# Layer 1 attention: mask, sink and row minimum in one VectorE instruction, no mask matmuls, exponential in place

## The chip, the cores and the metric

One core of a Trainium2 chip runs the whole program. The metric is the device time in microseconds (us) of one execution. The time before is the median of three runs; one further execution was taken with a profile, and its rows are the ones shown here.

## The reference, cut to what matters

Two layers work on 1024 latent tokens and 256 context tokens. The part that is changed is the attention of layer 1, for the latent tokens alone: 16 query heads share 4 key heads (64 wide), each block of 128 queries sees the 256 context tokens and a band of at most three blocks of 128 latent tokens, and every head has one more logit, the sink, that takes part in the softmax but has no value.

```python
valid = (jnp.abs(qpos[:, None] - kpos[None, :]) <= WINDOW) & (kpos[None, :] >= 0) & (kpos[None, :] < n)
s_loc = jnp.einsum('bqkgd,bskd->bkgqs', qi, kb).astype(jnp.float32) * scale
s_loc = jnp.where(valid, s_loc, -1e30)
s_ctx = jnp.einsum('bqkgd,bskd->bkgqs', qi, kc).astype(jnp.float32) * scale
p = jax.nn.softmax(jnp.concatenate([s_ctx, s_loc, sink_col], axis=-1), axis=-1).astype(v.dtype)
return (jnp.einsum('bkgqs,bskd->bqkgd', p[..., :L_ctx], vc)
        + jnp.einsum('bkgqs,bskd->bqkgd', p[..., L_ctx:L_ctx + 3 * BLOCK], vb))
```

## The kernel before

The attention is cut into 32 units: 8 query blocks (`i`) times 4 key heads (`kv`), and a unit has 4 query heads (`h`). In the 24 units of blocks 1 to 6 the band is three blocks wide, so that a head has 640 score columns; in the 8 units of blocks 0 and 7 it has 512.

The steps of a unit are short methods. `Q` transposes the queries on TensorE and `Qh` copies them to SBUF. `S` computes the scores of a head into PSUM: two products for the context columns, two for the band (the query is split in a high and a low part that lie under each other, and so are two versions of the keys), and then one or two products of the identity with a 128x128 mask `mkb` (0 or -1e30), which are accumulated onto the first and the last 128 band columns. `mx` takes the negated maximum of the scores (VectorE, reads PSUM) and then the minimum of that and the negated sink, in a 128x1 instruction. `e` is the exponential on ScalarE, from PSUM into the SBUF tile `P`, with the negated maximum as its bias and the row sum as a second output. `T` and `V` transpose `P` on TensorE; `hi` (ScalarE) and `lo` (VectorE) split the transposed tile into a high and a low part, `pt`; for the fifth 128 columns these steps are `vh` and `vl`. `AV` multiplies by the values, block by block, into one PSUM tile `po`, of which there is one buffer. `ob` and `ot` copy its two halves out (ScalarE), `ad` adds them (GpSimd), `se`, `ee` and `sum` make the reciprocal of the softmax's sum, `N` spreads it over 64 partitions by TensorE, and `mu` multiplies (VectorE).

The order of these steps is written out by hand: `SWA_ORDER` lists 45 steps with a shift each, and in every step of the loop the steps of the present unit (shift 0), the one before (1), and so on, are issued in that order. So every engine has a fixed queue, and the units overlap. A query block's `q_block` loads the queries (SyncE) and splits them on GpSimd (a copy of 1.0 us and a subtraction of 2.4 us); it is issued once in four units. Score tiles have two PSUM buffers, the small transposes two, `po` and the spread reciprocal one each. The tile `P` has five buffers, which the loads of keys and values at the stage's start use as well (`ks`).

Ahead of the units, ten tiles of keys and values are loaded and split, `mk` (the two masks) is loaded by one transfer and rounded to bf16 by ScalarE, and the sink is loaded and negated (`nsink`).

Of the kernel before, what the change touches and what calls it, by code (L numbers as in the profile page):

```python
# [9 lines left out]
F32 = mybir.dt.float32  # L10
QUEUES = {mybir.EngineType.PE, mybir.EngineType.Activation, mybir.EngineType.DVE, mybir.EngineType.Pool, mybir.EngineType.SP}
F32R = mybir.dt.float32r
BF16 = mybir.dt.bfloat16
I32 = mybir.dt.int32
U32 = mybir.dt.uint32
AF = mybir.ActivationFunctionType
ALU = mybir.AluOpType
AX = mybir.AxisListType
# [5 lines left out]
NC = 256  # L24
NT = NX + NC
TC = NC // 128
TX = NX // 128
# [70 lines left out]
def hybrid_block_kernel(ctx, tc, A, out, dbg=None, upto=99):  # L98
    nc = tc.nc
    dbg = dbg or {}  # L100
    pe, act, dve, pool, sp = nc.tensor, nc.scalar, nc.vector, nc.gpsimd, nc.sync
# [20 lines left out]
    def bank(tag, name):  # L122
        bufs, banks = cur["tags"][tag]
        return cur["p"].tile([128, 512 * banks], F32, tag=tag, bufs=bufs, name=name)
# [8 lines left out]
    identb = const.tile([128, 128], BF16, name="identb")  # L133
# [29 lines left out]
    def hilo(hi, lo, src):  # L163
        act.copy(hi, src)
        dve.tensor_sub(lo, src, hi.bitcast(F32))  # L165
# [580 lines left out]
    def layer0_mixer():  # L746
# [20 lines left out]
        with sbuf("l0a") as ap_, sbuf("l0t") as tp:  # L767
# [127 lines left out]
            with sbuf("l0b") as bp, psum("l0s", S=(2, 2), M=(1, 1), T=(2, 1), O=(1, 1)):  # L895
                class Pair:


                    def __init__(self, h, g):
                        self.h, self.g = h, g  # L900
                        self.mxm = bp.tile([128, 2], F32, tag="mx", bufs=4, name="mx")
                        self.sm = [bp.tile([128, 3], F32, tag="sm", bufs=8, name="sm") for _ in range(2)]
                        self.P, self.Sb, self.last, self.PT = {}, {}, {}, None

# [26 lines left out]
                    def probabilities(self, u):  # L931
                        if u not in self.P:
                            self.P[u] = bp.tile([128, NT], F32, tag="P", bufs=3, name="P")
                        return self.P[u]

# [13 lines left out]
                    def T(self, u, c):  # L949
# [5 lines left out]
                        for j in range(n):  # L955
                            pe.transpose(p[:, j * 128:(j + 1) * 128], self.P[u][:, (b0 + j) * 128:(b0 + j + 1) * 128], ident)  # L956
                        us = slice(u * 128, (u + 1) * 128)
# [38 lines left out]
                class Few(Pair):  # L996


                    def __init__(self, h):
                        self.h, self.g = h, 0  # L1000
                        self.mxm, self.sms = [bp.tile([128, 2], F32, tag=t, bufs=2, name=t) for t in ("fmx", "fsm")]
                        self.P = bp.tile([128, 2, NC], F32, tag="fP", bufs=1, name="fP")
                        self.PT = [bp.tile([128, TC, 256], F32R, tag=f"fpt{i}", bufs=1, name=f"fpt{i}") for i in range(2)]
# [940 lines left out]
    def layer1_mixer(st1, last, load_qkv, w_qkv, cols, x_first):  # L1944
# [199 lines left out]
        with sbuf("l1a") as ap_, sbuf("l1k", side="right") as kp, psum("l1s", S=(2, 2), B=(2, 1), O=(1, 1), R=(1, 1)):  # L2144
            kT = [ap_.tile([128, 4, NT], F32R, name=f"k1T{i}") for i in range(2)]
            V = []
            for t in range(TT):
                ks = ap_.tile([128, 640], F32, tag="P", bufs=5, name="ks1")[:, :512].rearrange("p (i h d) -> p i h d", i=2, d=64)
                sp.dma_start(ks, kvd[t * 128:(t + 1) * 128])
                v = ap_.tile([128, 4, 2, 64], F32R, name=f"V1_{t}")  # L2150
                pool.tensor_copy(v[:, :, 0, :], ks[:, 1])
                pool.tensor_sub(v[:, :, 1, :], ks[:, 1], v[:, :, 0, :].bitcast(F32))
                V.append(v)
                kk = ap_.tile([128, 5, 4, 128], F32R, tag=f"pt{t % 2}", bufs=2, name="kk")
                kk = kk.rearrange("p a b c -> p (a b c)")[:, :768].rearrange("p (a b c) -> p a b c", a=4, c=64)
                hilo(kk[:, :, 0, :], kk[:, :, 1, :], ks[:, 0])
                dve.tensor_copy(kk[:, :, 2, :], kk[:, :, 0, :].bitcast(F32))
                ts = slice(t * 128, (t + 1) * 128)
                for i in range(2):
                    p = bank("B", "pkt")  # L2160
                    for j in range(4):
                        pe.transpose(p[:, j * 128:(j + 1) * 128].bitcast(F32R),
                                     kk[:, j, i:i + 2, :].rearrange("p i d -> p (i d)"), identr)
                    (act.copy if i else dve.tensor_copy)(kT[i][:, :, ts], p.rearrange("p (h t) -> p h t", t=128))
            mk = kp.tile([128, 2, 128], F32, name="mk")
            sp.dma_start(mk, A["band"].rearrange("m p s -> p m s"))
            mkb = ap_.tile([128, 2, 128], BF16, name="mkb")
            act.copy(mkb, mk)
            sinkb = ap_.tile([128, 16], F32, name="sinkb")
            load_bcast(sinkb, A["swa_sink"], 0, 16)  # L2170
            nsink = ap_.tile([128, 16], F32, name="nsink")
# [12 lines left out]
            class Unit:  # L2184
# [18 lines left out]

                def Qh(self):
                    self.qT = ap_.tile([128, 4, 128], F32R, tag="qT", bufs=2, name="qT1")
                    act.copy(self.qT, self.qp.rearrange("p (h t) -> p h t", t=128))

                def S(self, h):
                    i, kv, nl, l0 = self.i, self.kv, self.nl, self.l0
                    p = self.Sb[h] = bank("S", "psc1")  # L2210
                    pc, pl = p[:, NC:512], p[:, 512:512 + nl]
                    q = self.qT[:, h, :]
                    for n in range(2):
                        pe.matmul(pc, q, kT[1 - n][:, kv, :NC], start=n == 0, stop=n == 1)
                    for n in range(2):
                        pe.matmul(pl, q, kT[1 - n][:, kv, l0:l0 + nl], start=n == 0, stop=False)
                    ms = ([(0, 0)] if i > 0 else []) + ([(1, nl - 128)] if i < TX - 1 else [])
                    for n, (w, c0) in enumerate(ms):
                        pe.matmul(pl[:, c0:c0 + 128], identb, mkb[:, w, :], start=False, stop=n == len(ms) - 1)

                def mx(self, h):
                    hd = self.kv * 4 + h
                    nm = self.nm[:, h:h + 1]
                    dve.tensor_reduce(nm, self.Sb[h][:, NC:NC + self.nk], axis=AX.X, op=ALU.max, negate=True)
                    dve.tensor_tensor(nm, nm, nsink[:, hd:hd + 1], op=ALU.min)

                def e(self, h):
                    P = self.P[h] = ap_.tile([128, 640], F32, tag="P", bufs=5, name="P1")
                    act.activation(P[:, :self.nk], self.Sb[h][:, NC:NC + self.nk], AF.Exp, bias=self.nm[:, h:h + 1],
                                   accum_out=self.sm[:, h:h + 1])  # L2230

                def T(self, h):
                    p = bank("B", "ppt1")
# [77 lines left out]
            with tc.manual_schedule():  # L2311
                q_block(0)
                for step in range(len(units) + depth):
# [8 lines left out]
                    for name, shift in SWA_ORDER:  # L2322
                        p = obj.get(step - shift)
# [62 lines left out]
    if upto < 5.5:  # L2386
        return
    pre = layer1_mixer(st1, lasts[0], load_qkv, w_qkv, cols, x_first)
    if upto < 7:
        return  # L2390
# [167 lines left out]
```

## Time and profile before

| | before |
|---|---|
| median of 3 runs | 2895.5 us (2894.02 to 2897.7) |
| the profiled execution | 2898.11 us, its span 2896.3 us |
| TensorE matmuls, share of the span | 92% |
| VectorE | 76% |
| ScalarE | 56% |
| GpSimd | 16% |
| first score product of layer 1's attention, last mask product | 1832.8 us, 2102.3 us |

The shares are means over stages with different limits, so what the change is worth must be read from its own stage, which takes about 9% of the span. The profiled execution took 2.6 us more than the median of the runs; differences worked out from its rows are taken off the median.

### The profile page before, as it was taken

To read this page: it belongs to the slowest core of one execution; us is meant where nothing else is said; L and a number is where in the kernel's file an instruction comes from. 1 tells how busy PE (TensorE), PEld (TensorE's weight loads), DVE (VectorE), ACT (ScalarE), POOL (GpSimd) and SP (SyncE) were. 2 spreads that over 40 slices of the span, in tenths; PEclk is the share of its full clock that TensorE was granted. 3 is DMA by queue.
4 is the path that set the end of the run, shared out by engine and by line. 5 is a ranking of instruction groups with operands and counts; after the bars stand their busy time and mean duration, and the time that the engine had idled before them with its cause. 6 is when DMAs were issued, how large, how long until landed. Compare 5 with 4: busy or idle time off the path is not lost.

```text
span 2896.3 us, 43462 instructions
## 1 busy us (share of the span) xinstructions
PE 2677.9 (92%) x16939; PEld 2152.5 (74%) x16939; DVE 2200.8 (76%) x3425; ACT 1620.5 (56%) x2443; POOL 449.8 (16%) x294
## 2 busy tenths in 40 slices
PE   7999899999879999999999899899988599999996
PEld 5989899987657777776767677688866488877775
DVE  4776799986776666666676586899966688888887
ACT  4201577773245555555555543689933476676664
POOL 2100000000012110201111300322101522221103
PEclk8999999999989999999999899799989799999998
DMA  7552000017468878787878374311056699999994
GB/s 269 195 176 95 5 9 10 10 61 251 143 226 311 297 266 288 277 283 279 296 271 290 133 268 149 114 45 36 16 192 241 212 383 383 383 381 377 368 354 144
DMA packets 277198, 614.44 MB, mean 212 GB/s; under 512 B 25320, under 2 KB 73184, under 8 KB 274944
## 3 DMA queue, kind: packets, MB, share of 16 engines
q1 hardware_dynamic: 261840, 567.91, 54.6%
q0 software_dynamic: 15008, 43.62, 5.7%
q8 instruction: 133, 2.18, 0.3%
q14 instruction: 73, 0.60, 0.1%
q10 hardware_dynamic: 144, 0.13, 0.0%
HBM read 549.94 MB, written 61.67 MB: 211 GB/s over the span
## 4 chain that ended last, share of the span: by engine, by line
PE 71%; DVE 7%; ACT 6%; issue 2%; DMA 1%; POOL 1%; SPq 0%; DVEq 0%; ACTq 0%; POOLq 0%
PE pw L1226 6%; PE pg L1786 4%; PE pu L1788 4%; PE pu L1789 4%; PE pu L1791 4%; PE pd L1878 4%; PE pd L1874 4%; PE pg L1790 4%; PE pg L1787 4%; PE pd L1875 4%; ACT wh L1100 3%; PE po L982 3%; PE po L2285 2%; PE ppt L956 2%; PE ptr L410 2%
## 5 line engine op out<-in xcount | busy, mean ns | idle before, releaser
L1101 DVE TENSOR_TENSOR wl<-raw,wh 128x2048 fp32r<-128x2048 f32 x385 | 868.2, 2282 | 293.6 <-ACT wh L1100 292.4
L1100 ACT CAST wh<-raw 128x2048 fp32r<-128x2048 f32 (+1 forms) x392 | 734.3, 1903 | 338.5 <-PE pg L1790 203.1
L1883 POOL DMA_INDIRECT acc_x<-yo,gp x30 | 116.4, 3879 | 695.1 <-DVE yo L1882 653.1
L1788 PE MATMUL pu<-wl,xh 128*128 128x512 f32 x512 | 204.3, 399 | 6.0 <-DVE wl L1101 5.9
L1786 PE MATMUL pg<-wl,xh 128*128 128x512 f32 x512 | 208.6, 407 | 0.0
L1787 PE MATMUL pg<-wh,xh 128*128 128x512 f32 x512 | 202.9, 396 | 0.0
L1791 PE MATMUL pu<-wh,xl 128*128 128x512 f32 x512 | 202.0, 395 | 0.0
L1790 PE MATMUL pg<-wh,xl 128*128 128x512 f32 x512 | 202.0, 394 | 0.0
L1789 PE MATMUL pu<-wh,xh 128*128 128x512 f32 x512 | 201.9, 394 | 0.0
L1874 PE MATMUL pd<-wl,hh 128*128 128x512 f32 x480 | 194.0, 404 | 3.7 <-ACT csl L1817 3.7
L1875 PE MATMUL pd<-wh,hh 128*128 128x512 f32 x480 | 192.0, 400 | 0.0
L1878 PE MATMUL pd<-wh,hl 128*128 128x512 f32 x480 | 150.8, 395 | 0.0
L168 PE MATMUL pc<-hT,wh 128*128 128x256 f32 x480 | 140.2, 292 | 5.5 <-ACT wh L503 3.7
L170 PE MATMUL pc<-hT,wl 128*128 128x256 f32 x480 | 137.6, 287 | 4.8 <-DVE wl L504 4.8
L169 PE MATMUL pc<-hT,wh 128*128 128x256 f32 x480 | 136.5, 284 | 0.0
L1786 PEld LDWEIGHTS pg<-wl,xh 128*128 128x128 f32 x512 | 96.5, 188 | 36.3 <-issue 12.5
L1788 PEld LDWEIGHTS pu<-wl,xh 128*128 128x128 f32 x512 | 96.5, 189 | 33.4 <-DVE wl L1101 11.8
L1795 ACT ACTIVATE sil<-pg 128x512 f32<-128x512 f32 x64 | 38.3, 599 | 144.7 <-PE pg L1790 144.7
L1811 PE MATMUL pcg<-raw,cT 128*32 128x256 f32 x2048 | 116.9, 380 | 0.1
L963 ACT CAST pt<-ppt 128x512 fp32r<-128x512 f32 (+1 forms) x192 | 95.0, 515 | 39.1 <-PE ppt L956 37.0
L967 DVE TENSOR_TENSOR pt<-ppt,pt 128x512 fp32r<-128x512 f32 (+1 forms) x192 | 110.6, 593 | 7.7 <-ACT pt L963 5.2
L1790 PEld LDWEIGHTS pg<-wh,xl 128*128 128x128 f32 x512 | 96.5, 188 | 23.2 <-DVE xl L165 0.4
(459 smaller groups left out, 6592.0 us busy)
## 6 DMA issues: line engine op xcount, KB each, us to landing
raw<-in_exp_w_gate_dram SPq DMA_DIRECT2D x128, 1024.0 KB
raw<-in_exp_w_up_dram SPq DMA_DIRECT2D x128, 1024.0 KB
raw<-in_exp_w_down_dram SPq DMA_DIRECT2D x128, 1024.0 KB
raw<-in_mod_w_dram SPq DMA_DIRECT2D x48, 1024.0 KB
yT<-yTd SPq DMA_DIRECT2D x17, 512.0 KB
acc_x<-xn SPq DMA_DIRECT2D x16, 512.0 KB
h2x<-h SPq DMA_DIRECT2D x16, 512.0 KB
raw<-in_w_in_dram SPq DMA_DIRECT2D x8, 768.0 KB
```

The lines of the kernel that those rows point to most:

```text
L1100: act.copy(wh[:, cs], raw[:, cs])
L1101: (eng or dve).tensor_sub(wl[:, cs], raw[:, cs], wh[:, cs].bitcast(F32))
L1226: pe.matmul(self.pp[n], a[:, k], b[k // 2][:, k % 2, ns], start=(k == 0 and i == 0), stop=(k == 7 and i == 2))
L1786: pe.matmul(pg, xh[:, k], gl[:, j], start=k == 0, stop=False)
L1787: pe.matmul(pg, xh[:, k], gh[:, j], start=False, stop=False)
L1788: pe.matmul(pu, xh[:, k], ul[:, j], start=k == 0, stop=False)
L1789: pe.matmul(pu, xh[:, k], uh[:, j], start=False, stop=False)
L1790: pe.matmul(pg, xl[:, k], gh[:, j], start=False, stop=k == 7)
L1791: pe.matmul(pu, xl[:, k], uh[:, j], start=False, stop=k == 7)
L1874: pe.matmul(pd[n], hh[k // 4][:, k % 4], w[2][:, k % 2, ns], start=k == 0, stop=False)
L1875: pe.matmul(pd[n], hh[k // 4][:, k % 4], w[1][:, k % 2, ns], start=False, stop=False)
L1878: pe.matmul(pd[n], hl[k // 4][:, k % 4], w[1][:, k % 2, ns], start=False, stop=k == 7)
```

## The change

The queries are copied to SBUF with a factor of -1, so that the scores are negated. The mask products are gone. `mx` is one call: it adds the negated mask (an f32 tile in SBUF that is 0 over all unmasked columns and 1e30 where masked) to the negated scores in PSUM, writes the sum to `P` in SBUF, and gives the minimum over the row and the negated sink. `e` is the exponential of the negated `P`, in place. `P` is therefore taken one step earlier, and has six buffers. Two masks are made ahead of the units (640 and 512 columns; block 0 takes the shorter one, block 7 the first 512 columns of the longer one): GpSimd zeroes, three transfers load the two triangles, GpSimd negates.

```diff
-                ks = ap_.tile([128, 640], F32, tag="P", bufs=5, name="ks1")[:, :512].rearrange("p (i h d) -> p i h d", i=2, d=64)
+                ks = ap_.tile([128, 640], F32, tag="P", bufs=6, name="ks1")[:, :512].rearrange("p (i h d) -> p i h d", i=2, d=64)
...
-            mk = kp.tile([128, 2, 128], F32, name="mk")
-            sp.dma_start(mk, A["band"].rearrange("m p s -> p m s"))
-            mkb = ap_.tile([128, 2, 128], BF16, name="mkb")
-            act.copy(mkb, mk)
+            masks = [kp.tile([128, 640 - 128 * n], F32, name=f"mask{n}") for n in range(2)]
+            for n, m in enumerate(masks):
+                pool.memset(m[:, :NC + 256 - 128 * n], 0.0)
+                sp.dma_start(m[:, NC + 256 - 128 * n:], A["band"][1])
+            sp.dma_start(masks[0][:, NC:NC + 128], A["band"][0])
+            for m in masks:
+                pool.tensor_scalar(m[:, NC:], m[:, NC:], -1.0, None, op0=ALU.mult)
...
-                    act.copy(self.qT, self.qp.rearrange("p (h t) -> p h t", t=128))
+                    act.activation(self.qT, self.qp.rearrange("p (h t) -> p h t", t=128), AF.Copy, scale=-1.0)
...
-                        pe.matmul(pl, q, kT[1 - n][:, kv, l0:l0 + nl], start=n == 0, stop=False)
-                    ms = ([(0, 0)] if i > 0 else []) + ([(1, nl - 128)] if i < TX - 1 else [])
-                    for n, (w, c0) in enumerate(ms):
-                        pe.matmul(pl[:, c0:c0 + 128], identb, mkb[:, w, :], start=False, stop=n == len(ms) - 1)
+                        pe.matmul(pl, q, kT[1 - n][:, kv, l0:l0 + nl], start=n == 0, stop=n == 1)
...
                 def mx(self, h):
                     hd = self.kv * 4 + h
-                    nm = self.nm[:, h:h + 1]
-                    dve.tensor_reduce(nm, self.Sb[h][:, NC:NC + self.nk], axis=AX.X, op=ALU.max, negate=True)
-                    dve.tensor_tensor(nm, nm, nsink[:, hd:hd + 1], op=ALU.min)
+                    P = self.P[h] = ap_.tile([128, 640], F32, tag="P", bufs=6, name="P1")
+                    dve.tensor_tensor_reduce(P[:, :self.nk], self.Sb[h][:, NC:NC + self.nk],
+                                             masks[0 if self.i else 1][:, :self.nk], 1.0, nsink[:, hd:hd + 1],
+                                             ALU.add, ALU.min, self.nm[:, h:h + 1])
...
                 def e(self, h):
-                    P = self.P[h] = ap_.tile([128, 640], F32, tag="P", bufs=5, name="P1")
-                    act.activation(P[:, :self.nk], self.Sb[h][:, NC:NC + self.nk], AF.Exp, bias=self.nm[:, h:h + 1],
-                                   accum_out=self.sm[:, h:h + 1])
+                    P = self.P[h][:, :self.nk]
+                    act.activation(P, P, AF.Exp, bias=self.nm[:, h:h + 1], scale=-1.0, accum_out=self.sm[:, h:h + 1])
```

How this moves instructions can be seen on three queues. TensorE before, in a unit in the middle of the stage, where the scores of a head (`psc`) are followed by a value product (`po`) and a transpose of `P` (`ppt`):

```order
L2214 MATMUL psc_19320<-k1T_16872,qT_19302 128x256
L2214 MATMUL psc_19320<-k1T_16871,qT_19302 128x256
L2216 MATMUL psc_19320<-k1T_16872,qT_19302 128x384
L2216 MATMUL psc_19320<-k1T_16871,qT_19302 128x384
L2219 LDWEIGHTS identb
L2219 MATMUL psc_19320<-mkb,identb 128x128
L2219 LDWEIGHTS identb
L2219 MATMUL psc_19320<-mkb,identb 128x128
L2285 MATMUL po_19278<-pt_19125,V_5_16980 128x512
L2285 MATMUL po_19278<-pt_19126,V_5_16980 128x512
L2235 MATMUL ppt_19332<-ident,P_19310 128x128 x4
```

The same place of TensorE's queue now:

```order
L2218 MATMUL psc_19114<-k1T_16872,qT_19097 128x256
L2218 MATMUL psc_19114<-k1T_16871,qT_19097 128x256
L2220 MATMUL psc_19114<-k1T_16872,qT_19097 128x384
L2220 MATMUL psc_19114<-k1T_16871,qT_19097 128x384
L2286 MATMUL po_18965<-pt_18822,V_5_16980 128x512
L2286 MATMUL po_18965<-pt_18823,V_5_16980 128x512
L2236 MATMUL ppt_19015<-ident,P_18980 128x128 x4
```

The two mask products and their two loads of the identity are gone, 224 of each in the stage; the rest keeps its order.

VectorE before, from the last head's maximum of one unit to the next maximum (`psc` are scores, `nm` the negated maximum, `pt` the low parts):

```order
L2224 TENSOR_REDUCE nm<-psc_18950 128x1
L2225 TENSOR_TENSOR nm<-nm,nsink 128x1
L2255 TENSOR_TENSOR pt_18878<-ppt_18944,pt_18877 128x4x128
L2255 TENSOR_TENSOR pt_18878<-ppt_18962,pt_18877 128x4x128
L2264 TENSOR_TENSOR se<-nm,nsink 128x4
L2270 TENSOR_TENSOR sm<-sm,se 128x4
L2271 RECIPROCAL sm<-sm 128x4
L2224 TENSOR_REDUCE nm<-psc_18980 128x1
L2225 TENSOR_TENSOR nm<-nm,nsink 128x1
```

The same place of VectorE's queue now:

```order
L2225 ISA P_18797,nm<-psc_18780,mask_17083,nsink 128x640
L2225 ISA nm 128x1
L2256 TENSOR_TENSOR pt_18714<-ppt_18774,pt_18713 128x4x128
L2256 TENSOR_TENSOR pt_18714<-ppt_18790,pt_18713 128x4x128
L2265 TENSOR_TENSOR se<-nm,nsink 128x4
L2271 TENSOR_TENSOR sm<-sm,se 128x4
L2272 RECIPROCAL sm<-sm 128x4
L2225 ISA P_18837,nm<-psc_18806,mask_17083,nsink 128x640
L2225 ISA nm 128x1
```

The one call stands in the queue as two instructions: the one that streams the scores and the mask, and one of 128x1 that writes the minimum. VectorE has two instructions per head as before, in the same places.

SyncE's queue of transfers at the stage's start (rows with - are before, with + now):

```order
 L2149 DMA ks_17041<-kvd 128x512
 L2149 DMA ks_17062<-kvd 128x512
-L2166 DMA mk<-in_band_dram 128x2x128
+L2168 DMA mask_17083<-in_band_dram 128x128
+L2168 DMA mask_17084<-in_band_dram 128x128
+L2169 DMA mask_17083<-in_band_dram 128x128
 L206 DMA sinkb<-in_swa_sink_dram 128x16
```

Three transfers of 64 KB stand where one of 128 KB stood, ahead of the first load of queries.

## Rows read from the trace of the kernel before

**Rows 1.** Blocks 1 to 6: busy us of PE, PEld, DVE, ACT, POOL; clock, DMA.
```profile
1872.00:2075.00 203.00, 195.74 (x1443) 164.80 (x1441) 197.02 (x444) 182.01 (x421) 51.73 (x36) 1.00 0.11 32
```

**Rows 2.** Chain of waits, 1989.30 to 1997.63 us (one unit): shares by line.
```profile
by line: PE po L2285 32.8%; PE ppt L2235 21.1%; PE psc L2216 16.9%; PE psc L2214 11.5%; PE psc L2219 6.1%; PE ppv L2244 5.6%; PE pr L2276 5.2%; PE pqT L2201 3.5%
```

**Rows 3.** What TensorE waited for, 1870 to 2070 us: total, times, longest.
```profile
PE ppt L2235 <- DVE pt L2255: 7.2, 7, 1.1
```

**Rows 4.** VectorE's timeline over the same unit: start, duration, line.
```profile
1989.64 0.15 DVE L2264 TENSOR_TENSOR se<-nm,nsink 128x4 f32<-128x4 f32 x1
...
1990.91 0.16 DVE L2225 TENSOR_TENSOR nm<-nm,nsink 128x1 f32<-128x1 f32 x1
1991.12 1.29 DVE L2255 TENSOR_TENSOR pt<-ppt,pt 128x512 fp32r<-128x512 f32 x2
...
1993.17 0.26 DVE L2225 TENSOR_TENSOR nm<-nm,nsink 128x1 f32<-128x1 f32 x1
1993.36 0.41 DVE L2255 TENSOR_TENSOR pt<-ppv,pt 128x256 fp32r<-128x256 f32 x1
...
1995.82 0.81 DVE L2224 TENSOR_REDUCE nm<-psc 128x1 f32<-128x640 f32 x1
1996.67 0.16 DVE L2225 TENSOR_TENSOR nm<-nm,nsink 128x1 f32<-128x1 f32 x1
1996.74 1.31 DVE L2255 TENSOR_TENSOR pt<-ppt,pt 128x512 fp32r<-128x512 f32 x2
1997.97 0.15 DVE L2264 TENSOR_TENSOR se<-nm,nsink 128x4 f32<-128x4 f32 x1
```

**Rows 5.** Timelines of GpSimd and VectorE around a wait of Rows 3.
```profile
1976.62 2.37 POOL L2181 TENSOR_TENSOR qq<-qt,qq 128x1024 fp32r<-128x1024 f32 x1
1977.55 1.46 DVE L2225 TENSOR_TENSOR nm<-nm,nsink 128x1 f32<-128x1 f32 x1
```

**Rows 6.** Timelines of GpSimd and VectorE in the expert layer of layer 0.
```profile
1592.59 4.64 POOL L1101 TENSOR_TENSOR wl<-raw,wh 128x2048 fp32r<-128x2048 f32 x1 [20.09 <-ACT wh L1100]
1595.20 0.69 DVE L1796 TENSOR_TENSOR sil<-sil,pu 128x512 f32<-128x512 f32 x1 [2.22 <-ACT sil L1795]
```

**Rows 7.** VectorE's timeline in the router, where an instruction has an accumulated output.
```profile
801.69 0.35 DVE L1627 TENSOR_SCALAR_CACHE_REDUCE rcm<-rval,rsc 128x128 f32<-128x128 f32 x1
801.96 0.08 DVE L1627 DVE_READ_ACCUMULATOR rcm<-rval,rsc 128x1 f32 x1
802.08 0.34 DVE L1629 TENSOR_SCALAR_CACHE_REDUCE rcm<-rval,rsc 128x128 f32<-128x128 f32 x1
```

**Rows 8.** Groups by line and shape, VectorE: busy us, mean ns.
```profile
L2224 DVE TENSOR_REDUCE nm<-psc 128x1 f32<-128x640 f32 x96 | 78.5, 818 | 1.1 <-PE psc L2219 0.3
L353 DVE SCALAR_TENSOR_TENSOR modacc<-raw,csil,modacc 128x1024 f32<-128x1024 f32 x56 | 68.3, 1278 | 0.0
L1882 DVE SCALAR_TENSOR_TENSOR yo<-pd,gp,g 128x512 f32<-128x512 f32 x60 | 42.1, 743 | 6.3 <-PE pd L1878 6.3
```

**Rows 9.** Groups by line and shape, ScalarE: from SBUF (L1241), from PSUM.
```profile
L2250 ACT CAST pt<-ppt 128x512 fp32r<-128x512 f32 x128 | 72.2, 587 | 12.6 <-PE ppt L2235 7.1
L1241 ACT ACTIVATE pw<-xn 128x512 f32<-128x512 f32 x36 | 21.7, 602 | 122.1 <-DVE xn L1235 122.0
```

**Rows 10.** Timelines of TensorE and ScalarE: the loop through the one `po` buffer.
```profile
1992.11 0.73 PE L2285 MATMUL po<-pt,V 128*128 128x512 f32 x2
1996.74 0.59 ACT L2250 CAST pt<-ppt 128x512 fp32r<-128x512 f32 x1 [0.20 <-PE ppt L2235]
1998.14 0.58 ACT L2290 COPY ob<-po 64x512 f32<-64x512 f32 x1
1998.83 1.08 ACT L2250 CAST pt<-ppt 128x512 fp32r<-128x512 f32 x2
1999.81 0.58 ACT L2294 COPY ot<-po 64x512 f32<-64x512 f32 x1
```

**Rows 11.** SyncE's queue at the stage's start.
```profile
1817.11 0.43 SPq L2166 DMA_DIRECT2D mk<-in_band_dram  x1
```

## The prediction

> **What bounds the kernel now.** I read the windows of the stage first, then the chain of waits over one unit, then what TensorE waited for, and last the timelines of VectorE and ScalarE.
>
> In blocks 1 to 6 of the attention TensorE is busy 195.74 of 203.00 us, VectorE 197.02, ScalarE 182.01, at the full granted clock (1.00, the 2.4 GHz level) [rows 1]. Two engines at 97% cannot be told apart by busy time. The chain can: one unit lasts 8.33 us (from one `se` to the next, 1989.64 to 1997.97 [rows 4]), and over such a stretch every piece of the chain is a TensorE product [rows 2]. So inside a unit TensorE is the bound, with VectorE close behind. Between units there is one repeated wait: 7 times in 200 us TensorE waits for a low part (`pt`) of VectorE, 7.2 us in all [rows 3]. Its origin is not the arithmetic: while GpSimd subtracts for `q_block` (1976.62 to 1978.99), the 128x1 minimum of `mx`, which has two operands in SBUF, takes 1.46 us and ends with it, against 0.16 us elsewhere [rows 4, 5].
>
> **TensorE.** The mask products are 6.1% of a unit's chain, 0.51 us [rows 2]. Without them TensorE's floor is 8.33 - 0.51 = 7.82 us per unit. If VectorE or ScalarE cannot follow, this gain stops at their floor.
>
> **VectorE.** What does a unit need? Its 8.33 us hold two short waits that the change does not need. A minimum lets the next instruction start 0.07 us later where nothing is in the way (1996.67 to 1996.74); it was 0.21 at 1990.91 and 0.19 at 1993.17 [rows 4]. So the need is 8.33 - 0.14 - 0.12 = 8.07 us. The pair of maximum and minimum holds VectorE 0.92 us (1995.82 to 1996.74).
>
> The new instruction is in no row of before. It has the shape of an operation on two tensors with one per-partition operand and an accumulated output, so I build it from two rows. The router's instruction with such an output shows a second row, the read of the accumulator, which starts 0.27 us after the first one, at 128 columns [rows 7]. A column more costs (1278 - 743) / 512 = 1.045 ns [rows 8], so 640 columns add 0.53 us: 0.80. From the accumulator's read to the next start the router has 0.12 us; the small instruction above has 0.07 [rows 4, 7]. That bounds the pair between 0.87 and 0.92 us at full rate. I take 0.88: the next instruction in the queue is a low part or another score row, and neither reads the minimum. The dearest reading at full rate adds whole rows without any overlap: 743 + 128 x 1.045 = 877 ns and 0.16 us, 1.04 us. With 0.88 VectorE's need becomes 8.07 - 4 x 0.04 = 7.91 us. This is the term on which most hangs: VectorE gains almost nothing from the fusion, because two instructions replace two, and the streaming one reads the same 640 columns.
>
> **ScalarE and the loop through `po`.** `po` has one buffer, so the first value product of a unit waits for `ot` of the unit before. The loop runs 1992.11 (first `po`) to 1996.74 (a `hi` that waited 0.20 us for TensorE), 4.63 us; from there 3.07 us to `ot` at 1999.81; `ot` itself 0.58 us and 0.05 us more to the next unit, 8.33 in all [rows 10]. Two of the four mask pairs lie in the first leg (`S3`, `S0`): 4.63 - 0.26 = 4.37. In the second leg `ob` holds ScalarE 0.69 us (1998.14 to 1998.83), though the copies after it follow each other in 0.49: a wait of 0.20 for the transposes behind `S1`, which come earlier too. The exponential reads SBUF now. The nearest rows are 602 against 587 ns at 512 columns, for different operations; I take 0.02 us [rows 9]. The loop becomes 4.37 + 2.89 + 0.63 = 7.89 us. ScalarE is at 90% in this stretch and the extra 4 x 0.02 us per unit lie in its idle time [rows 1]; with a factor of -1 in `Qh` and the in-place exponential nothing else changes there, and the rounding of the masks was ahead of the units.
>
> So there are three floors, 7.82, 7.91 and 7.89. Engines that hand work to each other this closely do not meet the highest floor exactly; I take 7.95 as an estimate. 24 units of three-block bands: 24 x (8.33 - 7.95) = 9.1 us.
>
> **The wait behind GpSimd.** The minimum that waited is gone. The new instruction reads one tensor from PSUM and one from SBUF. A row shows such an instruction beside GpSimd: `sil` times `pu` (PSUM) starts at 1595.20, inside a GpSimd subtraction that runs to 1597.23, and takes its normal 0.69 us [rows 6]. So I expect no wait. It is worth 7.2 us as TensorE's idle time [rows 3], or 7 x 1.30 = 9.1 us as VectorE's lost time [rows 5]; I take 8. The remaining operations on two SBUF tensors (`se` and the sum after it) stand later in a unit. The Trainium skill, page SBUF — State Buffer, section SBUF: two separate sides, says that VectorE and GpSimd share one pair of ports under an exclusive lock, and that VectorE needs it in a two-port mode or with two SBUF inputs. The trace agrees in both directions (1.46 us held, 0.69 us not held). No run here shows the case with a per-partition operand in SBUF beside the tensor in SBUF; if that counted as a second input, the wait would stay (a rival below).
>
> **At nothing.** Two more transfers are issued ahead of the first query load, 0.43 us each [rows 11], while six buffers instead of five let the last key loads start sooner; within 1 us either way. Zeroing and negating the masks is GpSimd work ahead of the units; if the first `mx` had to wait for it, that would be once. The six buffers cover that `P` is taken a step earlier: six allocations back, its readers `T` and `V` stand before `mx` in the order. The 8 units of the edge blocks lose one product per head, at most 4 x 0.065 = 0.26 us each where TensorE bounds them; no row here shows that, so it counts for the low end alone (2 us).
>
> **Sum.** 9.1 + 8 = 17.1 us. The profiled execution took 2898.1 us, which gives 2881.0; taken off the median of 2895.5 it is 2878.4, and I say 2878. What follows the stage starts when it ends, so I let the gain pass through whole.
>
> **Rivals.**
> - *VectorE becomes the bound.* If the pair costs 0.99 us or a little more, VectorE's need is 8.35 and the unit keeps its length; only the 8 us of the wait are gained: 2887.5. For it: no row shows this instruction, and the whole rows without overlap make 1.04 us. Against it: the queue overlaps neighbours everywhere else.
> - *The wait behind GpSimd stays*, on the new instruction: 9.1 us are left, 2886.4. For it: it reads two things in SBUF besides PSUM.
> - *Slower: the new instruction runs at half rate.* Then the pair is 0.88 + 0.67 = 1.55 us, VectorE needs 8.07 + 4 x 0.63 = 10.59 us, and 24 units cost 24 x 2.26 = 54 us more, less the 8: 2941. It turns from gain to loss where VectorE's need passes 8.33 + 8 / 24, at a pair of 1.07 us. Against it: an operation on three inputs, two of them f32 tensors in SBUF, does 1024 columns in 1278 ns, one column per 1.25 ns with all fixed cost [rows 8]; but it has no accumulated output, and the router's instruction that has one streams a single tensor. The Trainium skill, page Vector Engine (DVE) Microarchitecture Reference, section Points that are easy to get wrong, says that the form on two tensors loses half its rate with two non-bf16 sources in SBUF, as no read port is left for the accumulator. Here one source is in PSUM, so by the letter the rule does not bite.
> - *The gain is lost behind the stage*, in a transfer or a weight conversion that starts no earlier: 2895. The stage's transfers are few (DMA share 0.11 [rows 1]), which speaks against it.
>
> **How the numbers follow.** Forecast 0.57; VectorE bound 0.12; wait stays 0.12; half rate, or anything beyond the point of 1.07 us, 0.13; lost later 0.06. The forecast's own range is 2872 (units at TensorE's floor of 7.82, 12.2 us, the wait at 9.1, the edge at 2) to 2882 (pair at 0.92, 6.2 us, the wait at 7.2). To hold 8 in 10 the range takes in the first two rivals and a microsecond beyond either end: 2871 to 2889. A measurement tells about 0.2% (5.8 us) from no change. Faster is the forecast and the first two rivals, rounded down, 0.79; the same 0.08; slower 0.13.
>
> **What the profile after would show.** A unit's `se` to `se` of 7.9 to 8.0 us, in every unit, with no longer one in four; no mask rows; two rows per head on VectorE, the first near 0.85 us, the second near 0.1; the next start 0.88 us after the first. A first row near 1.5 us, or a second one that waits for GpSimd, would show the rivals. The prediction is wrong if the pair passes 1.07 us, or if the stage ends 17 us sooner and the program does not.

## The result and the profile after

The changed kernel takes **2872.8 us** (median of 4 runs, 2870.3 to 2877.3) against 2896.6 us for the kernel before in the same comparison (4 runs, 2894.0 to 2902.1). The ratio is 0.9917 with a 95% interval of 0.9898 to 0.9936: 24 us less. The forecast was 2878 with a range of 2871 to 2889, and faster as the likeliest sign. The sign was right, and both parts of the gain came; which engine holds a unit came out otherwise than forecast (below), and the gain was about 6 us larger. The profiled execution lasted 2877.3 us, its span 2875.3.

The windows of blocks 1 to 6, with the columns of [rows 1]:

```profile
1872.00:2050.00 178.00, 177.37 (x1205) 155.60 (x1205) 171.00 (x425) 174.59 (x403) 50.77 (x35) 1.00 0.12 37
```

TensorE has gone from 96% of the stretch to 99.6%, ScalarE from 90% to 98%, VectorE from 97% to 96%. The granted clock is the same (1.00). Busy shares this close do not tell which engine sets the pace; the experiments do.

VectorE's timeline over a unit that ran beside a GpSimd subtraction, the case of [rows 4, 5]:

```profile
1967.15 0.88 DVE L2225 CUSTOM_DVE_ANT_0 P<-psc,mask,nsink 128x640 f32<-128x640 f32 x1
1967.96 0.09 DVE L2225 DVE_READ_ACCUMULATOR2_ANT nm<- 128x1 f32 x1
1967.96 0.42 DVE L2256 TENSOR_TENSOR pt<-ppv,pt 128x256 fp32r<-128x256 f32 x1
1968.30 0.88 DVE L2225 CUSTOM_DVE_ANT_0 P<-psc,mask,nsink 128x640 f32<-128x640 f32 x1
1969.10 0.08 DVE L2225 DVE_READ_ACCUMULATOR2_ANT nm<- 128x1 f32 x1
1969.10 1.41 DVE L2256 TENSOR_TENSOR pt<-ppt,pt 128x512 fp32r<-128x512 f32 x2
1970.43 0.15 DVE L2265 TENSOR_TENSOR se<-nm,nsink 128x4 f32<-128x4 f32 x1
...
1971.56 0.08 DVE L2225 DVE_READ_ACCUMULATOR2_ANT nm<- 128x1 f32 x1
1971.85 1.29 DVE L2256 TENSOR_TENSOR pt<-ppt,pt 128x512 fp32r<-128x512 f32 x2 [0.20 <-ACT pt L2251]
...
1978.39 0.15 DVE L2265 TENSOR_TENSOR se<-nm,nsink 128x4 f32<-128x4 f32 x1
```

GpSimd's timeline at the same place:

```profile
1967.31 2.40 POOL L2184 TENSOR_TENSOR qq<-qt,qq 128x1024 fp32r<-128x1024 f32 x1
```

Three things are to be seen. The new instruction that starts at 1968.30, inside the subtraction (1967.31 to 1969.71), takes its normal 0.88 us: the wait of 1.46 us in [rows 5] is gone. The read of the accumulator starts 0.80 us after the instruction and the next one starts in the same hundredth of a microsecond, so a pair holds VectorE for 0.80 to 0.83 us, less than the 0.87 that was the lower bound. And `se` to `se` is 7.96 us (1970.43 to 1978.39), where [rows 4] had 8.33.

From the fourth `se` to the 28th (24 interior units) the trace has 191.04 us after and 208.55 before. All but the last (7.90) of these last 7.95 to 7.97 us; before, 17 lasted 8.2 to 8.4 and 7 some 9.5 to 9.65.

What VectorE and TensorE still wait for over the interior units (total, times, longest), to be held against [rows 3]:

```profile
DVE pt L2256 <- ACT pt L2251: 5.0, 24, 0.2
...
PE po L2286 <- ACT ot L2295: 0.5, 1, 0.5
...
PE ppv L2245 <- DVE pt L2256: 0.3, 1, 0.3
```

TensorE's 7.2 us have shrunk to under 1 us; VectorE now waits once in every unit, 0.2 us, for a high part from ScalarE.

### The profile page after: what moved, and what is told of

It is laid out like the page before. It is cut to its first block, busy times and chain, and to the rows that moved or that the text cites. A ratio compares the mean times of both kernels' runs of the same rounds, so it can differ in the third digit from the quotient of the medians.

```text
span 2875.3 us, 43000 instructions
## 1 busy us (share of the span) xinstructions
PE 2661.8 (93%) x16715; PEld 2148.5 (75%) x16715; DVE 2178.5 (76%) x3425; ACT 1621.2 (56%) x2442; POOL 457.2 (16%) x298
```

## The experiments

"24 units" is the time from the fourth `se` to the 28th in the profiled execution; where medians are given, the kernel before ran beside them on the same chip.

**The wait alone.** Edit of the kernel before:

```diff
-                    dve.tensor_tensor(nm, nm, nsink[:, hd:hd + 1], op=ALU.min)
+                    dve.tensor_scalar(nm, nm, nsink[:, hd:hd + 1], None, op0=ALU.min)
```

> The kernel before with the minimum of mx in the form with one tensor and a per-partition operand, in place of the form with two tensors; both operands still lie in SBUF. Theory (the repeated wait is that of two tensor inputs in SBUF): the 128x1 minimum takes about 0.1 to 0.2 us everywhere, none near 1.4 us, the 7.2 us of TensorE's waits for VectorE go, units 8.33 us throughout, 24 units about 200.5 us, median about 8 us under the kernel before. Rival (a per-partition operand in SBUF counts as a second input): minima of 1.4 us stay and nothing changes.

Measured: 2889.5 us against 2896.9, ratio 0.9975 (0.9965 to 0.9985), 24 units 199.76 us. The instruction's summary (count, then minimum, median and longest ns), first of the kernel before, then of this one:

```profile
L2225 DVE TENSOR_TENSOR nm<-nm,nsink x96: 158/160/1631, 1868.1 to 2074.1; 128x1 f32<-128x1 f32 x96
```

```profile
L2225 DVE TENSOR_SCALAR nm<-nm,nsink x92: 212/214/217, 1866.9 to 2057.2; 128x1 f32<-128x1 f32 x92
```

The form with one tensor never waits, though its per-partition operand lies in SBUF too: 12 of these minima start while GpSimd subtracts for `q_block`, and all 12 take 214 or 215 ns. In the kernel before, six minima started there, and each lasted until 0.02 us after the end of the subtraction. The one-tensor form costs 54 ns more, and the units are 8.31 to 8.35 us but for the first two and the last (8.21 to 8.26). So the wait was worth 8.8 us of stage (208.55 to 199.76), and it belonged to the form with two tensor operands, not to SBUF operands as such. The rival is out.

**The mask products alone.** Edit of the kernel before (the mask is missing in it):

```diff
-                        pe.matmul(pl, q, kT[1 - n][:, kv, l0:l0 + nl], start=n == 0, stop=False)
-                    ms = ([(0, 0)] if i > 0 else []) + ([(1, nl - 128)] if i < TX - 1 else [])
-                    for n, (w, c0) in enumerate(ms):
-                        pe.matmul(pl[:, c0:c0 + 128], identb, mkb[:, w, :], start=False, stop=n == len(ms) - 1)
+                        pe.matmul(pl, q, kT[1 - n][:, kv, l0:l0 + nl], start=n == 0, stop=n == 1)
```

> The kernel before with the mask products left out and nothing in their place, so the mask is left out. Theory (the gain per unit needs both parts: TensorE freed, and VectorE's pair a little cheaper): VectorE is the bound at its need of 8.07 us or a little more, an interior unit (se to se) is 8.07 to 8.15 us, units beside a q_block subtraction are still longer by about 1.3 us because the 128x1 minimum still waits for GpSimd; 24 units 208.5 - 24 x 0.2 = about 203 to 204 us, median about 5 us under the kernel before. Rival A (all of the unit's gain is TensorE's): 7.96 us and 24 units about 199 us, 9 us under. Rival B (VectorE alone was the bound before): 8.33 us, no change.

Measured: 2892.9 us, ratio 0.999 (0.9981 to 1.0), which alone cannot be told from no change. The trace can: quiet units are 8.14 to 8.21 us, those beside a subtraction 9.5, 24 units 205.25 us. The wait of 1.3 us stays. Three quiet units, with the columns of [rows 1]:

```profile
1946.30:1970.80 24.50, 24.46 (x163) 20.72 (x162) 23.85 (x59) 23.52 (x55) 3.84 (x3) 1.00 0.14 44
```

Their 8.15 us are not TensorE's need, though TensorE counts as busy for 99.8% of them: the changed kernel has the same products and takes 7.96. A busy TensorE thus may be waiting inside its products. ScalarE has no more to do here than in the changed kernel, so by exclusion these units are read as VectorE's (its need was forecast at 8.07). Of the 0.37 us per unit that the whole change brings, 0.18 come with the mask products gone; the other 0.19 need the cheaper VectorE pair as well.

**The mask products put back.** Edit of the changed kernel (a zero tile in `mkb`, the loop as in the diff above):

```diff
+                    for n, (w, c0) in enumerate(ms):
+                        pe.matmul(pl[:, c0:c0 + 128], identb, mkb, start=False, stop=n == len(ms) - 1)
```

> The changed kernel with as many mask products on TensorE as before, of a zero tile, added to the scores (they change no score). Theory: an interior unit is back at TensorE's 8.33 us, without the repeated wait, so 24 units take 24 x 8.33 = 200 us against 191.04 (changed) and 208.55 (before), as the kernel before with the other form of minimum has them (199.76); median about 9 us above the changed kernel, some 15 us under the kernel before. Rival (VectorE set a good part of the 8.33): units near 8.1 us, 24 units about 195.

Measured: 2886.1 us, ratio to before 0.9964 (0.995 to 0.9978), 24 units 199.92 us, units of 8.33 to 8.35 us but for the first two and the last (8.19 to 8.28). With these products TensorE is the bound again, although VectorE's pair is now the cheaper one; this kernel and the one with the other minimum meet at the same 200 us. The median lies about 13 us above the changed kernel's, 4 more than forecast from the units; the two medians are from different comparisons.

**What holds a unit at 7.96 us?** Three edits of the changed kernel, each of which lightens one engine, and two of them together. The exponential back to PSUM:

```diff
-                    dve.tensor_tensor_reduce(P[:, :self.nk], self.Sb[h][:, NC:NC + self.nk],
+                    dve.tensor_tensor_reduce(self.Sb[h][:, NC:NC + self.nk], self.Sb[h][:, NC:NC + self.nk],
...
-                    act.activation(P, P, AF.Exp, bias=self.nm[:, h:h + 1], scale=-1.0, accum_out=self.sm[:, h:h + 1])
+                    act.activation(P, self.Sb[h][:, NC:NC + self.nk], AF.Exp, bias=self.nm[:, h:h + 1], scale=-1.0, accum_out=self.sm[:, h:h + 1])
```

> The changed kernel with the one difference that the new VectorE instruction writes its sum back over the scores in PSUM, and the exponential reads PSUM and writes P. Theory A (ScalarE sets the 7.96 us of a unit: it is busy 195.38 of 200 us): the exponential is 797 ns again instead of 828, ScalarE has 4 x 0.03 = 0.12 us less per unit, and a unit falls to 7.84 to 7.88 us, 24 units about 188.5. Rival B (TensorE, or the hand-overs between engines, set it): 7.96 stays or grows. VectorE's instruction may last longer when it writes PSUM; that is not known, and above about 0.95 us it would hide the answer.

Measured: 2874.8 us, ratio to before 0.9922 (0.9906 to 0.9939), units of 7.93 us, 24 units 190.29 us. Groups by line, busy us and mean ns, of the changed kernel and then of this one:

```profile
L2225 DVE CUSTOM_DVE_ANT_0 P<-psc,mask,nsink 128x640 f32<-128x640 f32 x90 | 78.7, 874 | 0.7
L2231 ACT ACTIVATE P<-P,nm 128x640 f32<-128x640 f32 x90 | 74.5, 828 | 0.0
```

```profile
L2225 DVE CUSTOM_DVE_ANT_0 psc<-psc,mask,nsink 128x640 f32<-128x640 f32 x90 | 79.3, 881 | 0.0
...
L2231 ACT ACTIVATE P<-psc,nm 128x640 f32<-128x640 f32 x90 | 71.5, 795 | 0.0
```

ScalarE gets its 0.13 us per unit back (4 x 33 ns), VectorE hardly pays for writing PSUM (881 against 874 ns), but only 0.03 us arrive. That is nearer to theory B. By the medians a version that writes PSUM is not measurably better.

Without `ot` (its half of the value products is left out):

```diff
-                    act.copy(self.o2, self.po[:64, :])
...
-                    pool.tensor_add(self.o1, self.o1, self.o2)
+                    pool.tensor_add(self.o1, self.o1, self.o1)
```

> The changed kernel without the copy ot on ScalarE (GpSimd adds ob to itself in its place, so the lower half of the value products is left out of the output). Takes 0.59 us per unit off ScalarE and nothing off TensorE or VectorE. Theory A (ScalarE sets 7.96): the unit falls to TensorE's floor, 7.80 to 7.86 us. Rival B (TensorE with its hand-overs sets it): 7.92 to 7.97.

Measured in one execution: units 7.89 to 7.93 us (middle 7.91) but for the first and the last, 24 units 189.38 us. The copy lasts 0.59 us; ScalarE's busy time falls by 0.39 us per unit, since copies that follow each other overlap (two in 1.08 us, [rows 10]), and the unit by 0.05. Windows of the stage (PE, PEld, DVE, ACT, POOL):

```profile
1872.00:2050.00 178.00, 177.57 (x1216) 155.93 (x1215) 170.80 (x428) 166.88 (x384) 43.06 (x34) 1.00 0.12 37
```

ScalarE alone does not set 7.96: the result lies 0.01 below rival B's range and 0.05 above theory A's. The 0.05 us can be ScalarE's work or its hold on the one `po` buffer, as the edit takes away both. That TensorE has 99.8% of the stretch does not make 7.91 its floor (the quiet units without mask products had 99.8% at 8.15); the two edits together show it (below).

Half of the context scores left out:

```diff
-                        pe.matmul(pc, q, kT[1 - n][:, kv, :NC], start=n == 0, stop=n == 1)
+                        if n == 0:
+                            pe.matmul(pc, q, kT[1 - n][:, kv, :NC], start=True, stop=True)
```

> The changed kernel with one of the two 256-column products of the context scores left out per head (the low part of the context scores is missing). Takes 4 x 0.12 = about 0.5 us per unit off TensorE (a 128-column product was 0.064 us) and nothing off the others. Theory A (ScalarE sets 7.96): 7.90 to 7.96 us, hardly a change. Rival B (TensorE sets it): it falls until ScalarE's or VectorE's need holds it, 7.75 to 7.85.

Measured in one execution: units 7.86 to 7.90, 24 units 189.09 us; TensorE is down to 172.04 of 178 us, ScalarE up to 175.31. TensorE's busy time falls by 0.32 us per unit, the unit by only 0.08. The result lies between both theories: neither engine alone sets 7.96. Both lightened at once:

> The changed kernel without ot and with one of the two context score products left out (lower half of the value products and low part of the context scores are missing). TensorE then needs about 7.91 - 0.43 = 7.5 us and ScalarE about 7.3, so that VectorE's need shows. Theory (the new pair holds VectorE 0.80 to 0.83 us, as two starts in a row show it): 8.07 - 4 x 0.10 = 7.67, a unit of 7.6 to 7.75 us. Rival (0.88, as the prediction took it): 7.88 to 7.92.

Measured in one execution: 7.83 or 7.84 us in every interior unit but the first, 24 units 187.69 us. What VectorE waited for in the stage:

```profile
DVE pt L2257 <- ACT pt L2252: 4.8, 23, 0.2
```

This kernel differs from the one without `ot` in TensorE's work alone, and the unit falls from 7.91 to 7.83: so 7.91 was TensorE's. It differs from the one with half the context scores in `ot` alone, and the unit falls from 7.88 to 7.83: so 7.88 was ScalarE's, or that of its hold on `po`. What is left is read as VectorE's: without that one wait of 0.21 us a unit would be 7.62 us of VectorE work, where the pair of 0.80 to 0.83 us put it (7.6 to 7.75); but the wait stays when ScalarE is lightened, and 7.83 is between the two expectations. So the floors are 7.91 (TensorE), about 7.88 (ScalarE with `po`; ScalarE is at 98.5% there) and 7.83 (VectorE with its one hand-over), and the changed kernel runs at 7.96, 0.05 over the highest. Lightening one engine brought 0.05 or 0.08 us, two of them 0.13.

**The form with both sources in SBUF.** A second instruction of the new kind for the last head of each unit of the changed kernel:

```diff
+                    if h == 3:
+                        dve.tensor_tensor_reduce(P[:, :self.nk], P[:, :self.nk],
+                                                 masks[0 if self.i else 1][:, :self.nk], 1.0, nsink[:, hd:hd + 1],
+                                                 ALU.add, ALU.min, self.nm[:, h:h + 1])
```

> The changed kernel with a second instruction of the new kind for every fourth head, which reads P and the mask, both f32 in SBUF, and writes P (the mask is added twice there, which changes no weight). It measures the form with no source in PSUM. Theory by the rows of this kernel (full rate whatever the source): about 0.87 us like the one before it, VectorE needs some 8.4 to 8.5 us per unit, 24 units about 203. Rival (half rate with two f32 sources in SBUF, as the Trainium skill, page Vector Engine (DVE) Microarchitecture Reference, section Points that are easy to get wrong, has it for this kind of form): about 1.5 us, 9.1 us per unit, 24 units about 219. Both: it may wait where GpSimd subtracts, as the two-tensor minimum of the kernel before did, which the changed instruction does not.

Measured in one execution: 24 units 222.77 us, quiet units 8.81 and 8 of 24 about 10.2. Seven of the eight hold a wait of the second instruction behind GpSimd; in the eighth (2023.23 to 2033.39) there is none, and the granted clock is 0.90 from 2023 to 2033, where it is 1.00 from 2033 to 2043. By the sum alone this looks like the rival (219). The rows say otherwise; the instruction's summary, and VectorE's timeline beside a subtraction that ran from 1944.40 to 1946.78:

```profile
L2229 DVE CUSTOM_DVE_ANT_0 P<-P,mask,nsink x20: 884/886/2289, 1870.5 to 2047.8; 128x640 f32<-128x640 f32 x20
```

```profile
1944.25 0.89 DVE L2225 CUSTOM_DVE_ANT_0 P<-psc,mask,nsink 128x640 f32<-128x640 f32 x1
1945.06 0.08 DVE L2225 DVE_READ_ACCUMULATOR2_ANT nm<- 128x1 f32 x1
1945.17 2.29 DVE L2229 CUSTOM_DVE_ANT_0 P<-P,mask,nsink 128x640 f32<-128x640 f32 x1
```

```profile
1944.40 2.38 POOL L2184 TENSOR_TENSOR qq<-qt,qq 128x1024 fp32r<-128x1024 f32 x1
```

The median is 886 ns: full rate with two f32 sources in SBUF. The time came from elsewhere. The second instruction starts 0.11 us after the read of the first one's accumulator (1945.06 to 1945.17) and not with it; it reads the tile that the first one writes until 1945.14. The 7.62 us of VectorE work, the hand-over of 0.21, 0.89 and 0.11 make 8.83, beside 8.81 in the quiet units. And beside GpSimd the second instruction takes 2.29 us. The two rows side by side are the cleanest view of the wait in this study: the instruction with its scores in PSUM runs through the start of the subtraction at 0.89 us, the same instruction on two SBUF tensors ends 0.68 us after its end, about the time that its 640 columns need. The Trainium skill, page Vector Engine (DVE) Microarchitecture Reference, section Points that are easy to get wrong, has half the rate for a form on two tensors with two non-bf16 SBUF sources; the trace does not agree for this instruction (886 against 874 ns), if the page means it too. The Trainium skill, page SBUF — State Buffer, section SBUF: two separate sides, has a lock on the shared ports that VectorE needs for two SBUF inputs; this trace agrees (2.29 against 0.89 us).

**The start of the stage.** From the last `kvd` store to the first `se` the trace has 38.1 us before (1806.32 to 1844.42) and 34.9 after (1810.68 to 1845.61), where the prediction had nothing. First suspect, the sixth buffer (edit of the kernel before: `bufs=5` becomes `bufs=6` at both places):

> The kernel before with six P buffers in place of five, nothing else. Theory (the changed kernel's 3.2 us less from the last kvd store to the first se come from the key loads that can start sooner): that stretch falls from 38.1 to about 35 us, units unchanged at 8.33 with the repeated wait, median 2 to 3 us under the kernel before, which is at the edge of what the rounds tell. Rival (they come from the masks or from where the profiled executions began): 38.1 stays.

Measured: 2897.5 us, ratio 1.0003 (0.9993 to 1.0012), the stretch 37.2 us, 24 units 208.47. No change of the time that can be measured; 0.9 of the 3.2 us at most. Part of the rest shows in ScalarE's timeline, first before, then after:

```profile
1832.16 0.58 ACT L2206 CAST qT<-pqT 128x512 fp32r<-128x512 f32 x1 [0.44 <-PE pqT L2201]
1835.18 1.28 ACT L2229 ACT_TABLE_LOAD   x1 [2.43 <-DVE nm L2225]
1836.47 0.69 ACT L2229 ACTIVATE P<-psc,nm 128x512 f32<-128x512 f32 x1
```

```profile
1834.70 0.60 ACT L2209 ACTIVATE qT<-pqT 128x512 fp32r<-128x512 f32 x1 [0.44 <-PE pqT L2204]
1835.32 1.28 ACT L2231 ACT_TABLE_LOAD   x1
1837.51 0.72 ACT L2231 ACTIVATE P<-P,nm 128x512 f32<-128x512 f32 x1 [0.91 <-DVE nm L2225]
```

Before, the load of the exponential's table stands behind the wait for the first `nm`; after, it runs while the first scores are made. Is the form of `Qh` the reason? Edit of the kernel before with six buffers:

```diff
-                    act.copy(self.qT, self.qp.rearrange("p (h t) -> p h t", t=128))
+                    act.activation(self.qT, self.qp.rearrange("p (h t) -> p h t", t=128), AF.Copy, scale=1.0)
```

> The kernel before with six P buffers and with the copy of Qh written as an activation with the factor 1.0, nothing else. Theory (in the changed kernel the load of the exponential's table no longer stands behind the wait for the first nm because of the form of Qh): the load starts right after the first qT, 2.4 us sooner, the first exponential follows its nm without the 1.28 us of the load, and the stretch from the last kvd store to the first se falls from 37.2 (six buffers) to about 35.9 us. Rival (it is the new VectorE instruction that lets it go ahead): the load still waits for nm, 37.2 stays. The units stay at 8.33 with the repeated wait.

Measured in one execution: the load still waits 2.43 us for `nm`, the first `se` stands 39.2 us behind the store, and the execution takes 2898.8 us beside 2898.9. That theory falls. The queue itself shows a difference. ScalarE's instructions of the exponential's line at this place (count, then minimum, median and longest ns, and the start), first before, then after:

```profile
L2229 ACTq EVENT_SEMAPHORE  x1: 38/38/38, 1835.1 to 1835.1; - x1
L2229 ACT ACT_TABLE_LOAD  x1: 1283/1283/1283, 1835.2 to 1835.2; - x1
L2229 ACT ACTIVATE P<-psc,nm x1: 687/687/687, 1836.5 to 1836.5; 128x512 f32<-128x512 f32 x1
```

```profile
L2231 ACT ACT_TABLE_LOAD  x1: 1283/1283/1283, 1835.3 to 1835.3; - x1
L2231 ACT ACTIVATE P<-P,nm x1: 722/722/722, 1837.5 to 1837.5; 128x512 f32<-128x512 f32 x1
```

Before, an instruction that only waits (`EVENT_SEMAPHORE`) stands ahead of the load; in the trace it waits for VectorE and TensorE, and the exponential itself waits for GpSimd. After, the exponential waits for VectorE alone, has that wait on itself, and nothing stands ahead of the load. It is the same in the other kernels: the four others with the old instruction and a late load have the extra wait, and all with the new instruction have none.

And what is the early load worth? Edit of the kernel before:

```diff
+            warm = ap_.tile([128, 1], F32, name="warm")
+            act.activation(warm, nsink[:, 0:1], AF.Exp)
```

> The kernel before with one 128x1 exponential into a scratch tile behind the negated sink, ahead of the units, nothing else. Theory (1.3 to 1.5 us of the changed kernel's shorter start come from the load of the exponential's table, which no longer stands between the first nm and the first exponential): the load stands at the scratch exponential, the first exponential of a unit follows the first nm without it, and the stretch from the first qT to the first se falls from 12.3 us (12.26, 12.29, 12.41, 12.53 and 12.82 in five kernels with the load behind the wait) to about 11.0, where the changed kernel and its variants have it (10.91, 11.26, 11.27). Rival (the shorter start comes from the new VectorE instruction itself): 12.3 stays. The units stay as before.

Measured in one execution: first `qT` at 1840.68, first `se` at 1851.73, 11.05 us, as expected. The load behind the wait costs 1.2 us here (12.26 to 11.05), once. The execution as a whole took 2905.5 us beside 2899.0, in which the later start of the stage (last `kvd` store at 1814.62) weighs most; in 13 profiled executions with the same instructions up to there, that store lies anywhere from 1806.3 to 1814.6.

## Why the prediction was right

**What bounds the kernel.** Right: TensorE inside a unit, VectorE close behind (8.33 with the mask products, 8.15 without), and one repeated wait. Only six of the seven waits stand beside `q_block`; the seventh (the minimum at 1916.72) stands beside another GpSimd subtraction of the same shape, 1915.79 to 1918.16. The account of the wait does not change by it.

**TensorE's floor** was mis-sized: the chain's 6.1% made 0.51 us and 7.82. The mask products cost 0.43 us, from 8.34 (products put back) to 7.91 (no `ot`); the chain's share overstated them a little.

**VectorE's pair** was taken at 0.88, bounded by 0.87 and 0.92. The dearest reading's first row was right (877 ns worked out, 874 measured), and so was the accumulator's read 0.80 us after its start. The error is the start of the next instruction: it follows the read at once, so the pair is 0.80 to 0.83 where nothing else holds the next instruction, and the work of a unit 7.62 instead of 7.91. Almost all of that is hidden behind the other two floors.

**ScalarE** was taken to have idle time for the exponential from SBUF (0.02 us; measured 0.03, 828 against 797 ns). That idle time closed as the units got shorter: 98% busy. Together with its hold on `po` it has 0.05 us of the unit (7.96 to 7.91 without `ot`); the loop through `po`, put at 7.89, was not measured by itself.

**The unit** was taken as 7.95, just above three near floors of 7.82, 7.91 and 7.89; it is 7.96, above 7.91, about 7.88 and 7.83. That the highest floor is 7.91 in both lists is luck: the prediction had VectorE there and TensorE at 7.82, and the runs have TensorE at 7.91 and VectorE at 7.83, so two errors of 0.09 and 0.08 cancelled. The judgement that three close floors leave a little on top was right. The 24 units gave 8.7 us (199.76 to 191.04) against 9.1.

**The wait behind GpSimd** gave 8.8 us against 8 (7.2 to 9.1). Together 17.5 against 17.1.

**At nothing** was the step that was too small. The edge blocks gave 2.1 us (22.49 to 21.28 and 30.49 to 29.55, between the outer `se`), which the prediction had named at 2 and kept for the low end. The number fits better than its reason, the lost products: without the mask products alone the edges fall by only 0.8 us (to 22.05 and 30.14), with the new instruction alone by 0.7 (to 22.13 and 30.18); as inside, both were needed. The start gave 3.2 us against "within 1 us": 1.3 from the first `qT` on (12.3 to 10.9), by the table load, which the prediction did not look at (1.2 where the load alone was moved); and 1.8 ahead of it, in the key loads and copies (25.8 to 24.0). The sixth buffer may explain about 1 of that, but the 13 executions spread from 24.0 to 26.4, those with six buffers just as widely, so the 1.8 are not shown to be a gain. In this pair of traces 17.5 + 2.1 + 3.2 = 22.8 us, beside 23.8 in the medians.

**The gain passes through whole**: right. From the last `se` to the end of the span it is 790.4 us before, 787.8 after, and 787.8 to 790.4 in all the others. The span fell by 21.0 us only, because this execution's stage began 4.4 us later, in parts that are the same.

**The rivals.** VectorE as the bound: the pair is 0.17 us below the point at which it would have been. The wait on the new instruction: not there, since its scores come from PSUM; with both tensors in SBUF it would have stayed. Half rate: not seen in either form. Lost behind the stage: no.

What stays open: why the table load went ahead of the wait in every kernel with the new VectorE instruction. Neither `Qh` nor the buffers do it. The queues suggest that the number of engines that the exponential waits for decides, three before and one after, but no run changes that alone.

## What to carry to other kernels

A per-partition minimum on two SBUF tensors cost 1.3 us more here beside a GpSimd subtraction of 128x1024; the same operation with the second operand as a per-partition scalar, or fused into an instruction that reads its scores from PSUM, did not wait. Before fusing such work, try the one-line change of form: here it gave 8.8 of the 22.8 us by itself.

Where the floors of three engines stand within 2% of each other, taking work from one of them is worth little: the 0.37 us per unit needed both the mask products off TensorE and a cheaper pair on VectorE; the first by itself gave half, the second nothing. Read such floors from runs that lighten one engine, not from busy shares.

Add up a stage from its edges too, and look where each engine's first use of a function stands: here a table load of 1.28 us behind a wait cost 1.2 us more than one ahead of it.

## What the runs showed of the hardware that was not expected

- The accumulator's read of the new instruction (83 ns) costs VectorE nothing where the next instruction does not need its result: the two start together (1967.96 and 1967.96). In the router of [rows 7] there were 0.12 us between them, and 0.11 where the next instruction read the tile just written.
- The new instruction takes 874 ns at 128x640 with one source in PSUM, 881 when it also writes PSUM, 886 with both sources in SBUF: where the tensors lie changes it by at most 12 ns, but it decides on the wait beside GpSimd (2289 ns).
- A 128x1 minimum takes 160 ns with two tensors and 214 ns with a per-partition scalar; the slower form made the kernel faster.
